# One macaron block on one core: the pool of norm vectors is opened before the two pools of split activations

## The chip, the core and the metric

The kernel runs on one core of a Trainium2 chip. The metric is device time in microseconds (us). The kernel before was run three times: 2274.84, 2276.01 and 2279.90 us, median 2276.01. A further execution was profiled; it took 2277.5 us, of which the profile's span of the program is 2275.7 us.

On this core PE multiplies matrices: a *stationary* operand of 128x128 is loaded into it (a weight load, PEld in the profile) and a *moving* operand of up to 512 columns streams past it. DVE, ACT and POOL work elementwise, SP issues DMAs. All five have their operands in the on-chip memory SBUF, in which a tile is a run of bytes at one address in each of 128 partitions; matmul results go to PSUM.

## The reference

For a float32 sequence of 1024 positions with 1024 features the reference computes one block:

```python
x = x + 0.5 * _swiglu(_rmsnorm(x, ffn1_norm[l]), ffn1_wg[l], ffn1_wu[l], ffn1_wd[l])
h = _rmsnorm(x, mix_norm[l])
proj = h @ w_in[l]
...
merged = gates[:, :, 0] * (y_a @ w_branch[l, 0])
... # the same for y_b, y_c, y_d
x = x + merged @ w_out[l]
x = x + 0.5 * _swiglu(_rmsnorm(x, ffn2_norm[l]), ffn2_wg[l], ffn2_wu[l], ffn2_wd[l])
```

`_swiglu` is `(silu(x @ wg) * (x @ wu)) @ wd` with 2816 inner features. `y_a` to `y_d` are four sequence mixers of width 256 (a gated linear recurrence in chunks, a retention, a windowed attention, and a convolution with a linear recurrence), each with its own projections in `w_in`; the rest of `w_in` gives the four gates.

## The kernel before

Every large product is made in three matmuls. A float32 operand is split into `hi`, the operand rounded to the type that PE multiplies fast (ACT), and `lo`, the rest (DVE or POOL); then hi·hi, hi·lo and lo·hi are summed in PSUM. Features lie in partitions, positions in columns, in two halves of 512 columns (q = 0, 1). One matmul has a 128x128 stationary piece of a weight and 512 columns of an activation as moving operand.

The program has three parts, one after the other.

- **FFN1** (class `Ffn`). The gate and up products are done by a scheme of seven block products instead of eight; their names are A11, A12, S2, S1, S4, A22 and S3 (`one`, lines 1160 to 1162). For each of 22 blocks of inner features, each name takes 4x3 matmuls; PE runs them in the order A11, S2, A12, S1, S4, A22, S3. The left operands (`xc_tiles`) of A11 and A12 lie in pool `h0`, those of S2 and S1 in pool `h1`, those of S4, A22 and S3 in pool `xc`. Weights come by DMA into `raw` and are split into `rg`, `rt`, `ru` and `v`. The finished activations are written to memory outside the core and come back for the down product (`down`, lines 1331 to 1333), both of whose split operands lie in `rg`, `rt` and `ru`; there 16 of the 24 raw weight loads go into `h0` and `h1`, since their left operands are dead by then.
- **The mixers and gates** (`mix`). The normed activation `h` (tiles nm0 and nm1, hi and lo) fills `h0` and `h1`. `unit` (lines 215 to 217) is 24 matmuls with a `w_in` piece from `rg`/`rt` as stationary and an `h` tile as moving operand. There are 56 pieces, each for both halves: 24 projections, then 32 gate pieces, each gate unit followed by 6 matmuls `wb` (lines 954 to 956) on the mixer's output, whose tiles lie in pools y0 and y1. The mixers themselves are generators in a background list: after each sixth matmul of a unit the list is ticked, and a generator whose count has run out issues its next step, with small matmuls of its own, between the unit's.
- **The output product and FFN2.** `product` (lines 260 to 262) multiplies the merged result, split again into `h0` and `h1`, by `w_out`: 384 matmuls with an `h0`/`h1` tile as moving operand. FFN2 is as FFN1.

PE's order is that of the code. The order of the other engines is that in which the pool and semaphore layer of the framework puts the program.

A pool is a stretch of SBUF; pools are stacked in the order in which they are opened. `const` starts at byte 16,512 of a partition and holds 2,176 bytes by the end (a packed table of 384, two columns of 64, three 128x128 tables of 512 each, 128 of derived vectors). `h0` and `h1` have eight buffers of 4,096 bytes each, so 65,536 together. `norm` holds the short vectors of the three norms: three tags (`rs_v`, `rs_y`, `rs_t`) of two buffers of 64 bytes, 384 in all. Then come `raw`, `rg` and `rt`, and after them the pools of each part. A tile of these has 4,096, 2,048 or 1,024 bytes, each a multiple of 512, so all tiles of one pool start at the same byte modulo 512:

| pool | starts at byte | modulo 512 |
|---|---|---|
| `const` | 16,512 | 128 |
| `h0`, `h1` | 18,688 | 256 |
| `norm` | 84,224 | 256 |
| `raw`, `rg`, `rt` | 84,608 | 128 |
| `v`, `t`, `s`, `xc`, `ru`, `tt`, `a`, `u`, `scale` of an FFN | 121,472 and up | 128 |
| y0, y1, merged, gate (with `wb`'s weights) | 144,000 and up | 128 |

Inside the pools of the four mixers some tiles are shorter, and their starts stand at other values (160, 224, 416 and more).

Of the kernel before, what the change touches and what calls it, by code (L numbers as in the profile page):

```python
# [34 lines left out]
class Weights:  # L35


    def __init__(self, nc, ahead):
        self.nc, self.ahead, self.alloc = nc, ahead, None
        self.src, self.got, self.lo_engine = [], {}, []  # L40
        self.issued = 0
# [51 lines left out]
class Net:  # L93
    def __init__(self, ctx, tc, a, cols):
        self.tc, self.nc, self.a = tc, tc.nc, a
        pool = lambda name, **kw: ctx.enter_context(tc.tile_pool(name=name, **kw))
        self.cpool = pool("const", bufs=1)
        self.hpools = [pool("h0", bufs=8), pool("h1", bufs=8)]
        self.npool = pool("norm", bufs=1)
        self.wide = {k: pool(k, bufs=b, reuse_waits="tile") for k, b in {"raw": 3, "rg": 4, "rt": 2}.items()}  # L100
        self.w, self.wo = Weights(self.nc, 2), Weights(self.nc, 2)
        self.w.alloc = self.wo.alloc = self.weight
        self.bg = Background()
        nc = self.nc
        self.small = self.const("small")
        self.mean_col = self.column("mean_col")
        nc.gpsimd.memset(self.mean_col, 1.0 / D)
        self.cols = cols
        self.eps = self.column("eps")
        nc.gpsimd.memset(self.eps, EPS)  # L110
# [1474 lines left out]
```

## Time and profile before

| | |
|---|---|
| median of three runs | 2276.01 us |
| the profiled execution | 2277.5 us, its span 2275.7 us |
| PE busy | 2220.4 us, 98% of the span, 10144 matmuls |
| PE weight loads busy | 1779.5 us, 78% |
| DVE busy | 1379.8 us, 61% |
| ACT busy | 875.5 us, 38% |
| POOL busy | 327.9 us, 14% |
| DMA queue q1 | 243.44 MB, 32% of 16 engines' span |

FFN1 takes the first 693 us, the projections run to 1011 us, the gates to 1523, the output product to 1612, FFN2 to the end. The ends of matmuls are modelled and overlap the next one's start, so how fast PE goes is read from the starts: the distance between the starts of two matmuls, divided by the number of matmuls between them.

### The profile page before, as it was taken

To read this page: it belongs to the slowest core of one execution; us is meant where nothing else is said; L and a number is where in the kernel's file an instruction comes from. 1 tells how busy PE (TensorE), PEld (TensorE's weight loads), DVE (VectorE), ACT (ScalarE), POOL (GpSimd) and SP (SyncE) were. 2 spreads that over 40 slices of the span, in tenths; PEclk is the share of its full clock that TensorE was granted. 3 is DMA by queue.
4 is the path that set the end of the run, shared out by engine and by line. 5 is a ranking of instruction groups with operands and counts; after the bars stand their busy time and mean duration, and the time that the engine had idled before them with its cause. 6 is when DMAs were issued, how large, how long until landed. Compare 5 with 4: busy or idle time off the path is not lost.

```text
span 2275.7 us, 26198 instructions
## 1 busy us (share of the span) xinstructions
PE 2220.4 (98%) x10144; PEld 1779.5 (78%) x10144; DVE 1379.8 (61%) x1925; ACT 875.5 (38%) x1154; POOL 327.9 (14%) x227
## 2 busy tenths in 40 slices
PE   6899999999999999999999999999999999999999
PEld 5688888887777777787777777888778888888777
DVE  8787777776673436314355233035788787777764
ACT  6232233233443533316477454133433333223332
POOL 0000000000003435223343344321100000000000
PEclk8999999999999999999999999999999999999999
DMA  3233232394333122231111222115223232348432
GB/s 142 93 102 106 86 111 91 124 325 149 106 125 112 53 75 78 77 117 65 58 54 45 74 72 88 47 47 181 79 93 115 93 116 93 116 135 318 139 115 93
DMA packets 115196, 245.10 MB, mean 108 GB/s; under 512 B 11264, under 2 KB 23168, under 8 KB 115072
## 3 DMA queue, kind: packets, MB, share of 16 engines
q1 hardware_dynamic: 115072, 243.44, 32.0%
q8 instruction: 79, 1.29, 0.2%
q14 instruction: 45, 0.37, 0.1%
HBM read 181.00 MB, written 62.39 MB: 107 GB/s over the span
## 4 chain that ended last, share of the span: by engine, by line
PE 91%; DVE 6%; ACT 2%; issue 1%; DMA 0%; POOL 0%; SPq 0%; DVEq 0%; ACTq 0%; POOLq 0%
PE X L1162 3%; PE X L1160 3%; PE X L1161 3%; PE S1p L1160 2%; PE S2p L1162 2%; PE S1p L1162 2%; PE S1p L1161 2%; PE S2p L1161 2%; PE S2p L1160 2%; PE S4p L1161 2%; PE S4p L1160 2%; PE S4p L1162 2%; PE S3p L1162 2%; PE S3p L1161 2%; PE A22p L1161 2%; PE S3p L1160 2%
## 5 line engine op out<-in xcount | busy, mean ns | idle before, releaser
L56 POOL TENSOR_TENSOR wlo<-raw,whi 128x1024 fp32r<-128x1024 f32 x56 | 136.4, 2438 | 258.3 <-ACT whi L55 246.7
L1011 ACT ACTIVATE uhi<-gu 128x1024 fp32r<-128x1024 f32 x44 | 46.7, 1062 | 276.4 <-PE S3p L1161 134.4
L55 ACT ACTIVATE whi<-raw 128x1024 fp32r<-128x1024 f32 x72 | 76.0, 1057 | 186.4 <-PE o L261 23.5
L964 DVE TENSOR_TENSOR gt<-gt,wb 128x512 f32<-128x512 f32 x48 | 32.9, 686 | 139.8 <-PE wb L956 80.0
L1011 ACT ACTIVATE ghi<-gu 128x1024 fp32r<-128x1024 f32 x44 | 46.7, 1060 | 164.4 <-DMA gu<-wgu 129.8
L191 POOL TENSOR_TENSOR nm0lo<-res,nm0hi 128x1024 fp32r<-128x1024 f32 x2 | 4.9, 2444 | 648.9 <-ACT nm0hi L190 648.9
L1160 PE MATMUL X<-A11hi,ghi 128*128 128x512 f32 x176 | 71.1, 404 | 9.3 <-ACT ghi L1011 9.3
L965 POOL TENSOR_TENSOR m<-m,gt 128x512 f32<-128x512 f32 x48 | 62.3, 1299 | 122.6 <-DVE gt L964 121.7
L1012 DVE TENSOR_TENSOR dloS<-wd,dhiS 128x1024 fp32r<-128x1024 f32 (+1 forms) x36 | 43.1, 1196 | 59.6 <-ACT dhiS L1011 59.6
L1160 PE MATMUL X<-A12hi,ghi 128*128 128x512 f32 x176 | 70.8, 402 | 7.7 <-ACT t L1170 7.7
L1162 PE MATMUL X<-A11hi,glo 128*128 128x512 f32 x176 | 71.5, 406 | 6.6 <-DVE glo L1012 6.6
L1011 ACT ACTIVATE dhiA<-wd 128x1024 fp32r<-128x1024 f32 (+1 forms) x36 | 35.6, 990 | 107.3 <-PE Ad L1332 53.4
L1011 ACT ACTIVATE dhiS<-wd 128x1024 fp32r<-128x1024 f32 (+1 forms) x36 | 35.6, 989 | 106.9 <-PE Dd L1332 39.1
L1162 PE MATMUL S2p<-S2hi,tlo 128*128 128x512 f32 x176 | 70.2, 399 | 4.2 <-DVE tlo L1012 4.2
L1206 ACT ACTIVATE a<-a 128x1024 f32<-128x1024 f32 x44 | 46.7, 1062 | 65.3 <-DVE a L1205 65.3
L1160 PE MATMUL S1p<-S1hi,thi 128*128 128x512 f32 x176 | 70.7, 402 | 0.0
L1161 PE MATMUL X<-A11lo,ghi 128*128 128x512 f32 x176 | 70.5, 401 | 0.0
L1162 PE MATMUL S1p<-S1hi,tlo 128*128 128x512 f32 x176 | 70.5, 400 | 0.0
L1161 PE MATMUL S1p<-S1lo,thi 128*128 128x512 f32 x176 | 70.4, 400 | 0.0
L1161 PE MATMUL X<-A12lo,ghi 128*128 128x512 f32 x176 | 70.4, 400 | 0.0
L1198 DVE TENSOR_TENSOR a<-S3p,a 128x512 f32<-128x512 f32 x44 | 30.4, 691 | 66.0 <-PE S3p L1162 66.0
L1332 PE MATMUL Ad<-aloA,dhiA 128*128 128x512 f32 x176 | 68.7, 390 | 1.6 <-DVE aloA L1012 1.6
(1209 smaller groups left out, 6895.1 us busy)
## 6 DMA issues: line engine op xcount, KB each, us to landing
gu<-wgu SPq DMA_DIRECT2D x92, 512.0 KB, 3.6
raw<-w_in SPq DMA_DIRECT2D x56, 512.0 KB, 3.5
acts<-s SPq DMA_DIRECT2D x88, 256.0 KB, 2.8
wd<-wd SPq DMA_DIRECT2D x40, 512.0 KB, 6.5
inS<-acts SPq DMA_DIRECT2D x40, 512.0 KB, 3.7
acts<-a SPq DMA_DIRECT2D x66, 256.0 KB, 3.3
inA<-acts SPq DMA_DIRECT2D x30, 512.0 KB, 3.7
res<-x SPq DMA_DIRECT2D x16, 512.0 KB, 7.1
```

The lines of the kernel that those rows point to most:

```text
L55: nc.scalar.activation(hi, raw, AF.Copy)
L56: getattr(nc, self.lo_engine[i]).tensor_tensor(lo, raw, hi.bitcast(F32), op=ALU.subtract)
L964: nc.vector.tensor_tensor(g, g, ps, op=ALU.mult)
L965: nc.gpsimd.tensor_tensor(m, m, g, op=ALU.add)
L1011: self.nc.scalar.activation(hi, src, AF.Copy)
L1012: self.nc.vector.tensor_tensor(lo, src, hi.bitcast(F32), op=ALU.subtract)
L1160: mm(ps, whi[:, s], hi, start=start and k == 0, stop=False, skip_group_check=True)
L1161: mm(ps, whi[:, s], lo, start=False, stop=False, skip_group_check=True)
L1162: mm(ps, wlo[:, s], hi, start=False, stop=k == 3, skip_group_check=True)
L1198: V.tensor_tensor(g[:, 1], ps, g[:, 1], op=ALU.add)
L1206: nc.scalar.activation(g, g, AF.Silu)
L1332: mm(outs[t], whi[:, j, m], alo[:, j], start=False, stop=False, skip_group_check=True)
```

## The change

One line moves: the pool `norm` is opened before `h0` and `h1` instead of after them.

```diff
         self.cpool = pool("const", bufs=1)
+        self.npool = pool("norm", bufs=1)
         self.hpools = [pool("h0", bufs=8), pool("h1", bufs=8)]
-        self.npool = pool("norm", bufs=1)
         self.wide = {k: pool(k, bufs=b, reuse_waits="tile") for k, b in {"raw": 3, "rg": 4, "rt": 2}.items()}
```

In the built program `norm` then starts at byte 18,688 and `h0` at 19,072, which is 128 modulo 512; `raw` and everything behind it keep their addresses. The instructions of all five engines are the same, in the same order and with the same waits. Only the addresses of tiles in `h0`, `h1` and `norm` differ: the first two by +384 bytes, the last by -65,536.

## Rows read from the trace of the kernel before

**Rows 1.** The page, parts 1 and 4: busy time; the chain that ended last.

```profile
PE 2220.4 (98%) x10144; PEld 1779.5 (78%) x10144; DVE 1379.8 (61%) x1925; ACT 875.5 (38%) x1154; POOL 327.9 (14%) x227
...
PE 91%; DVE 6%; ACT 2%; issue 1%; DMA 0%; POOL 0%; SPq 0%; DVEq 0%; ACTq 0%; POOLq 0%
```

**Rows 2.** Windows: stretch, length, busy us (instructions) by engine, granted clock, DMA share, GB/s.

```profile
0.00:105.00 105.00, 78.53 (x314) 62.28 (x314) 87.25 (x149) 54.58 (x69) 0.34 (x6) 0.89 0.32 115
105.00:470.00 365.00, 364.21 (x1580) 296.63 (x1581) 286.18 (x357) 106.59 (x131) 0.00 (x0) 1.00 0.34 116
...
693.00:1011.00 318.00, 313.88 (x1654) 246.11 (x1655) 125.56 (x258) 110.67 (x154) 117.74 (x73) 0.99 0.24 80
1011.00:1523.00 512.00, 511.68 (x2449) 399.95 (x2448) 182.93 (x337) 256.92 (x399) 185.21 (x138) 1.00 0.20 63
1523.00:1612.00 89.00, 89.00 (x383) 71.65 (x382) 46.74 (x50) 35.55 (x43) 11.89 (x5) 1.00 0.47 151
1612.00:1690.00 78.00, 70.71 (x321) 57.28 (x321) 68.10 (x91) 33.43 (x39) 5.13 (x2) 0.98 0.25 82
```

**Rows 3.** Timeline of PE in FFN1's gate and up: start us, us, instruction.

```profile
299.07 0.40 PE L1160 MATMUL S2p<-S2hi,thi 128*128 128x512 f32 x1
...
304.67 0.40 PE L1160 MATMUL S1p<-S1hi,thi 128*128 128x512 f32 x1
304.91 0.39 PE L1161 MATMUL S1p<-S1lo,thi 128*128 128x512 f32 x1
305.13 0.40 PE L1162 MATMUL S1p<-S1hi,tlo 128*128 128x512 f32 x1
...
307.47 0.39 PE L1160 MATMUL S4p<-S4hi,uhi 128*128 128x512 f32 x1
...
310.20 0.39 PE L1160 MATMUL A22p<-A22hi,vhi 128*128 128x512 f32 x1
...
315.64 0.40 PE L1160 MATMUL X<-A11hi,ghi 128*128 128x512 f32 x1
```

**Rows 4.** Timeline of PE in a gate unit and its wb.

```profile
1426.09 0.40 PE L215 MATMUL gb1q<-nm0hi,whi 128*128 128x512 f32 x1
...
1431.68 0.39 PE L954 MATMUL wb<-ybhi,wbhi 128*128 128x512 f32 x1
...
1433.06 0.40 PE L215 MATMUL gb1q<-nm1hi,whi 128*128 128x512 f32 x1
```

**Rows 5.** Timeline of PE in the output product.

```profile
1550.21 0.40 PE L260 MATMUL o<-mhi,whi 128*128 128x512 f32 x1
...
1560.01 0.40 PE L260 MATMUL o<-mhi,whi 128*128 128x512 f32 x1
```

**Rows 6.** Timeline of PE in FFN2's down product.

```profile
2102.63 0.39 PE L1331 MATMUL Bd<-ahiS,dhiS 128*128 128x512 f32 x1
...
2116.23 0.39 PE L1331 MATMUL Bd<-ahiS,dhiS 128*128 128x512 f32 x1
```

**Rows 7.** Window of one period of gate and up, PE alone: PE busy, granted clock, DMA.

```profile
300.00:318.90 18.90, 18.90 (x83) 1.00 0.24 71
```

**Rows 8.** Tiles S1lo and S3lo: PE's matmuls that read them, ns min/median/max.

```profile
L1161 PE MATMUL S1p<-S1lo,thi x176: 390/395/628, 45.5 to 2047.5; 128*128 128x512 f32 x176
...
L1161 PE MATMUL S3p<-S3lo,uhi x176: 389/389/389, 60.5 to 2055.6; 128*128 128x512 f32 x176
```

**Rows 9.** Waits of PE: waited for, us in total, times, longest.

```profile
PE vtr L419 <- DVE vst L412: 3.1, 1, 3.1
```

**Rows 10.** Groups of DVE by form, splits into h1 and xc: busy us, mean ns.

```profile
L1012 DVE TENSOR_TENSOR S1lo<-n1x,S1hi 128x1024 fp32r<-128x1024 f32 x2 | 2.4, 1219 | 0.0
...
L1012 DVE TENSOR_TENSOR S3lo<-n0x,S3hi 128x1024 fp32r<-128x1024 f32 x2 | 2.4, 1222 | 1.2 <-ACT S3hi L1011 1.2
```

**Rows 11.** Tile wd: what its readers waited for (us, times); its DMAs' landing.

```profile
  DMA wd<-wd: 0.7, 2
...
DMA to landing us min/median/max: 2.9/6.0/10.3
```

## The prediction

> **What bounds the kernel now.** I read the page first, then windows by stage, then PE's timeline in one place of each kind of product, and last the waits. The page says that PE is the bound: busy for 98% of the span, and 91% of the chain that ended last is PE [rows 1]. The windows say the same of each stage: PE fills 364 of 365 us of the steady gate and up, all but 0.3 us of the 512 us of gates and all 89 us of the output product, while DVE, the next busiest, has 286 of 365 us in the first of these [rows 2]. So nearly all of the time is a number of matmuls times the distance between their starts, and the question is only whether that distance depends on an address.
>
> The timeline answers it for the layout of before. In one period of gate and up, 36 matmuls of S2, A12 and S1 go from 299.07 to 307.47 us, 233.3 ns each; the 24 of A22 and S3 go from 310.20 to 315.64 us, 226.7 ns each [rows 3]. [...] The change of pace sits at the change of pool: S4, whose moving operand is in `xc` too, is the transition, 12 matmuls in 2.73 us or 227.5 ns. The other stages fall on the same two values. A gate unit, moving operand in `h0`/`h1`: 24 matmuls in 5.59 us, 232.9 ns; the six of `wb` behind it, all operands at 128: 1.38 us, 230.0 ns, a run too short to settle [rows 4]. The output product, moving operand in `h0`/`h1`: 42 in 9.80 us, 233.3 ns [rows 5]. The down product, all operands at 128: 60 in 13.60 us, 226.7 ns [rows 6]. The durations in the trace say it of all 176 matmuls of a group: S1lo has a median of 395 ns, S3lo is 389 at its least, median and most [rows 8].
>
> **The change part by part.** No instruction is added, removed or moved, and no wait; three pools change addresses, and each use of them is priced by itself.
>
> *Matmuls with a moving operand in `h0` or `h1`.* Of gate and up there are 4 names x 12 matmuls x 22 blocks x 2 FFNs = 2112; of units 56 x 2 x 24 = 2688; of the output product 384. Together 5184, half of the 10144. With `h0` and `h1` at 128, each of them has the residues that A22, S3 and the down product have now, so I give each their 226.7 ns.
>
> - Gate and up: 6.6 ns each. About 4 in 7 of the 635 matmuls in the two opening stretches (to 105 us, and from 1612 to 1690 us), some 360, gain nothing, since there PE is busy for only 78.5 of 105 and 70.7 of 78 us and waits for splits and norms, which do not become faster [rows 2]. That leaves 1750 x 6.6 ns = 11.6 us, and S4's transition adds 528 x 0.8 ns = 0.4 us. 12.0 us.
> - Units: 2688 x 6.2 ns = 16.7 us, and `wb` 64 x 6 x 3.3 ns = 1.3 us. Background work is issued behind at most every sixth matmul of a unit; a matmul with a small one next to it has no such distance to lose. I take half of these places as used and strike a twelfth: 16.5 us.
> - Output product: 384 x 6.6 ns = 2.5 us.
>
> The sum is 31.0 us. Struck from it: PE waits 3.1 us for a copy on DVE in front of a transpose [rows 9]. This wait ends when a chain on ACT, DVE and POOL ends, so what PE gains in the 40 us before it (some 170 matmuls x 6.2 ns = 1.0 us) only makes it longer. 30.0 us remain. Other waits of the mixers could grow as well, since their steps are spaced by counts of matmuls, and 36 matmuls become 0.2 us shorter. PE shows almost no waits there now: the gates' stage idles for 0.3 us in 512 [rows 2], so I take 0; with ends: none, or 30 places x 0.2 us = 6 us. A gain from this is excluded, as no step comes later.
>
> *DVE, ACT and POOL on tiles in `h0` and `h1`.* A split into `h1` takes DVE 1219 ns, one into `xc` 1222 ns [rows 10]: no difference between the residues. 0 us.
>
> *DMAs into `h0` and `h1`.* Of 48 loads of down weights, 32 go there. They land in 6.0 us at the median, and their readers sat idle for them for 0.7 us in all [rows 11]. I take 0; should they become slower, the down product's splits would be late first, and a twentieth on each landing (32 x 0.3 us = 10 us) would still be spread over loads that wait for nobody. With ends: -0.7 us, or +2 us if a fifth of it came through. [...]
>
> *Norm vectors.* They are a few columns wide and keep their residues. 0 us.
>
> [...]
>
> So the profiled execution of 2277.5 us would become 2247.5 us. The median of the runs shown is 1.5 us under that execution; from it, 2246 us.
>
> **The rivals.**
>
> *The pool matters, not the residue.* `h0` and `h1` are also the two pools lowest in the memory, and no other long moving operand lies there. If the 6 ns belong to that place, nothing happens: 2276 us, the change doing what it says to addresses and nothing to time. For it: the trace has no matmul of this shape at the bottom with residue 128, or higher up with 256. Against it: `h0` and `h1` reach over 64 KB and show one pace from end to end, and operands as far apart as `rg` (97 KB) and the FFN pools (from 121 KB) show another; a border just at the end of `h1` would be a coincidence. 7%.
>
> *The background work becomes the bound in the mixers.* The steps' spacing shrinks and PE runs into ACT and DVE chains; half of the units' 16.5 us is given back as waits in front of small matmuls, the time is 2254 us. For it: one such wait is there already [rows 9]. Against it: DVE has 126 of 318 and 183 of 512 us to do there [rows 2]. 8%.
>
> *The pairs lock in the slow step.* With `h` tiles the starts lie alternately 0.24 and 0.22 to 0.23 us apart [rows 3], as if each second matmul met something. If equal residues at the bottom of the memory made every matmul meet it, each of some 5000 would take up to 0.24 us, 6.7 ns more than now: +33 us, 2309 us. The point from which it decides is a mean distance in the units above 233 ns. Against it: all three products with equal residues show no alternation. 3%.
>
> **How the numbers follow.** The forecast (all `h` matmuls at the faster pace) has 82%, the rivals 7, 8 and 3%. The forecast's own spread is from 2241 us (nothing struck: 34.9 us) to 2252 us (6 us of grown waits). The second rival lies just above. A range from 2239 to 2258 us holds the forecast and the second rival but for their tails; the first and the third, 10%, stay outside. About 0.2% (4.5 us) is what a measurement of this kernel can tell from no change: faster has 90%, same 7%, slower 3%.
>
> **What would show it.** In the changed kernel's trace the groups S1p, S2p and X should have matmuls of 389 ns without spread; 36 matmuls from S2 to S4 should take 8.16 us instead of 8.40, a unit 5.44 instead of 5.59 us, 42 of the output product 9.52 instead of 9.80. The down product and A22/S3 should not change. PE's wait for the transpose should grow by about 1 us. If the distances in `h` products stay at 233 ns the first rival holds; if they fall and the gain is under 25 us, the waits of PE between 693 and 1523 us tell where it went. The prediction is wrong if the time is above 2258 us.

## The result, and the profile after

The changed kernel takes 2253.93 us (median of 4 runs, 2247.8 to 2257.39) against 2276.67 us (4 runs, 2274.84 to 2279.9): a ratio of 0.9896, interval 0.9870 to 0.9922. In the profiled executions the span goes from 2275.7 to 2254.2 us, 21.5 us less where 30 were forecast. The rest of the document is about these two numbers: with the time at the lower clock taken out 30.0 us are there, if not in the places where the sum had them, and 8.5 us go back to TensorE's clock. One of the 26 executions of the kernel before, beside the later experiments, took 12540 us; the ratios leave it out.

First the pace. PE's timeline of the changed kernel, the stretches of [rows 3 to 5] (start us, us, instruction):

```profile
295.76 0.39 PE L1160 MATMUL S2p<-S2hi,thi 128*128 128x512 f32 x1
...
303.92 0.39 PE L1160 MATMUL S4p<-S4hi,uhi 128*128 128x512 f32 x1
...
306.64 0.39 PE L1160 MATMUL A22p<-A22hi,vhi 128*128 128x512 f32 x1
...
312.08 0.39 PE L1160 MATMUL X<-A11hi,ghi 128*128 128x512 f32 x1
...
1416.75 0.39 PE L215 MATMUL gb1q<-nm0hi,whi 128*128 128x512 f32 x1
...
1422.19 0.39 PE L954 MATMUL wb<-ybhi,wbhi 128*128 128x512 f32 x1
...
1423.55 0.39 PE L215 MATMUL gb1q<-nm1hi,whi 128*128 128x512 f32 x1
...
1539.83 0.39 PE L260 MATMUL o<-mhi,whi 128*128 128x512 f32 x1
...
1549.35 0.39 PE L260 MATMUL o<-mhi,whi 128*128 128x512 f32 x1
```

The 36 matmuls from S2 to S4 take 8.16 us (8.40 in [rows 3]), the 24 of a unit 5.44 us (5.59 in [rows 4]), its `wb` 1.36 us (1.38), and 42 of the output product 9.52 us (9.80 in [rows 5]): 226.7 ns each. The 24 of A22 and S3 stay at 5.44 us. The spread of single durations has gone as well; the tiles S1lo and S3lo, ns min/median/max, against [rows 8]:

```profile
L1161 PE MATMUL S1p<-S1lo,thi x176: 387/389/628, 47.7 to 2025.9; 128*128 128x512 f32 x176
...
L1161 PE MATMUL S3p<-S3lo,uhi x176: 389/389/389, 59.5 to 2034.1; 128*128 128x512 f32 x176
```

Now what speaks against 30 us. The windows of the changed kernel, some of the stretches of [rows 2] (length; busy us and instructions of PE, PEld, DVE, ACT, POOL; granted clock, DMA share, GB/s):

```profile
105.00:470.00 365.00, 364.32 (x1607) 301.69 (x1608) 291.07 (x363) 108.76 (x134) 0.00 (x0) 1.00 0.36 121
693.00:1011.00 318.00, 313.24 (x1660) 247.44 (x1659) 123.61 (x256) 112.14 (x155) 116.32 (x73) 0.98 0.24 78
1011.00:1523.00 512.00, 511.35 (x2486) 406.62 (x2485) 187.12 (x340) 257.66 (x401) 184.52 (x139) 1.00 0.20 65
1612.00:1690.00 78.00, 75.07 (x335) 62.19 (x334) 64.79 (x92) 28.89 (x35) 0.00 (x0) 0.94 0.22 74
```

In steady gate and up, PE gets 1607 instructions done in 365 us where it did 1580, and in the gates 2486 where it did 2449. From 693 to 1011 us it is 1660 against 1654, hardly more, at a clock of 0.98 instead of 0.99. Windows of PE alone show where the clock was low; first before, then the changed kernel (PE busy us, granted clock):

```profile
693.50:697.00 3.50, 3.01 (x8) 0.61 0.92 264
1642.90:1646.00 3.10, 3.10 (x11) 0.54 0.00 0
1691.00:1694.50 3.50, 3.50 (x10) 0.52 0.60 177
```

```profile
654.90:661.60 6.70, 6.00 (x14) 0.50 0.63 188
781.20:784.50 3.30, 3.30 (x9) 0.50 0.04 16
859.70:863.00 3.30, 3.30 (x10) 0.50 0.44 117
900.70:904.00 3.30, 3.30 (x9) 0.50 0.45 164
1610.60:1614.00 3.40, 3.40 (x10) 0.50 0.00 0
1627.70:1634.30 6.60, 6.60 (x22) 0.50 0.00 0
```

In both traces the records of the granted clock hold 1.00 and 0.50 alone; they give these places 10.2 us at 0.50 before and 27.3 us after (the windows of before begin a little ahead of them, which is why they do not show 0.50; those of after lie inside them). The openings of the program, up to 75 us, have another 23.9 us of it in both. The timeline around the second place shows what PE did before the fall and what the low level costs:

```profile
776.09 0.39 PE L217 MATMUL p7q<-nm0hi,wlo 128*128 128x512 f32 x1
779.71 0.66 PE L419 MATMUL vtr<-c_ident,vst 128*128 128x128 f32 x4 [3.23 <-DVE vst L412]
...
781.55 0.63 PE L217 MATMUL p7q<-nm1hi,wlo 128*128 128x512 f32 x1
781.98 0.63 PE L215 MATMUL p7q<-nm1hi,whi 128*128 128x512 f32 x1
...
785.45 0.39 PE L216 MATMUL p7q<-nm1lo,whi 128*128 128x512 f32 x1
785.68 0.39 PE L217 MATMUL p7q<-nm1hi,wlo 128*128 128x512 f32 x1
```

PE idles for 3.23 us in front of the transpose, and 1.4 us after it has resumed the clock falls. The matmuls then start 0.43 us apart instead of 0.23. So a stretch at a granted clock of 0.50 in which PE has work costs about half its length. Ahead of the third place (the fourth reads alike) there is next to no wait, but a run of small matmuls:

```profile
855.84 0.39 PE L217 MATMUL p12q<-nm1hi,wlo 128*128 128x512 f32 x1
856.16 0.66 PE L488 MATMUL o<-Aatt,Av 128*64 128x128 f32 x8
856.65 0.26 PE L493 MATMUL o<-Aqbx,S 128*64 128x32 f32 x4
857.07 2.76 PE L493 MATMUL o<-Aqbx,S 128*64 128x32 f32 x27 [0.16 <-DVE S L475]
```

The wait for the transpose has grown, by 0.7 us where 1.0 was forecast ([rows 9]: 3.1 us, once):

```profile
PE vtr L419 <- DVE vst L412: 3.8, 2, 3.2
```

PE runs the same 10144 matmuls in the same order in both traces, so that stretches between equal matmuls can be compared. After minus before: FFN1's steady gate and up -6.1 us, the four groups of gates -2.4, -1.2, -2.1 and -2.7 us, the output product -2.6 us, FFN2's steady gate and up -7.4 us (1.5 us of it the fall at 1691 us, which only before has), both down products 0.0 us up to F, the last of FFN1's. Against that stand +2.8 us in F (the place at 655 us, 6.8 us of low clock), +1.5 us from the first `vtr` to p8 (781 us), +2.0 us in p12 (859 us) and +1.8 us in p15 (901 us). FFN2's opening stays as long as it was, with 10.2 us of low clock (1611 and 1628 us) where before had 3.4 us (1643 us).

### The profile page after: what moved, and what is told of

Read it like the earlier page. It is cut to its first block, busy times and chain, and to the rows that moved or that the text cites. A ratio compares the mean times of both kernels' runs of the same rounds, so it can differ in the third digit from the quotient of the medians.

```text
span 2254.2 us, 26198 instructions
## 1 busy us (share of the span) xinstructions
PE 2199.1 (98%) x10144; PEld 1783.1 (79%) x10144; DVE 1379.3 (61%) x1925; ACT 875.2 (39%) x1154; POOL 328.2 (15%) x227
## 4 chain that ended last, share of the span: by engine, by line
PE 88%; DVE 7%; ACT 3%; issue 1%; DMA 1%; POOL 0%; SPq 0%; DVEq 0%; ACTq 0%; POOLq 0%
PE X L1162 3%; PE X L1160 3%; PE X L1161 3%; PE S2p L1162 2%; PE S1p L1160 2%; PE S1p L1162 2%; PE S4p L1160 2%; PE S1p L1161 2%; PE S4p L1161 2%; PE S4p L1162 2%; PE S2p L1160 2%; PE S2p L1161 2%; PE S3p L1162 2%; PE A22p L1162 2%; PE S3p L1160 2%; PE A22p L1160 2%
## 5 line engine op out<-in xcount | busy, mean ns | idle before, releaser
L1160 PE MATMUL X<-A11hi,ghi 128*128 128x512 f32 x176 | 71.3, 405 | 10.2 <-ACT ghi L1011 10.2
L1162 PE MATMUL X<-A12hi,glo 128*128 128x512 f32 x176 | 69.7, 396 | 0.0
L1160 PE MATMUL S2p<-S2hi,thi 128*128 128x512 f32 x176 | 69.2, 393 | 0.0
```

The source lines that it names most:

```text
L1160: mm(ps, whi[:, s], hi, start=start and k == 0, stop=False, skip_group_check=True)
L1162: mm(ps, wlo[:, s], hi, start=False, stop=k == 3, skip_group_check=True)
```

## The experiments

half, all256, resid_a and vtr_later ran on one chip beside 9 runs of the kernel before (median 2276.93 us), resid_b, before_vtr and after_again on another beside 13 (2277.03 us). A mean distance of a name is taken from the start of its first matmul to the start of the next name's, over all periods of a steady stretch.

**half: one of the two pools.** The order of pools becomes `h1`, `norm`, `h0`; A11, A12 and nm0 live in `h0`, which now starts at 128 modulo 512, S1, S2 and nm1 in `h1`, which stays at 256.

```diff
-        self.hpools = [pool("h0", bufs=8), pool("h1", bufs=8)]
+        h1 = pool("h1", bufs=8)
         self.npool = pool("norm", bufs=1)
+        self.hpools = [pool("h0", bufs=8), h1]
```

> The changed kernel with h1 opened ahead of norm and h0 behind it: h0 at 128 modulo 512, h1 left at 256, everything else as before. Theory A (PE's pace depends on the starts of the moving and stationary operand modulo 512): products with operands in h0 (A11, A12, nm0 units, output product q=0) go at 227 ns from start to start, those in h1 (S2, S1, nm1 units, output product q=1) stay at 233 ns, and the time is halfway, about 2265 us (2276.7 before, 2253.9 with both). Theory B (the gain comes from something else that the move did, as the norm vectors' place or the order of the three pools): no such split between h0 and h1, both at 227 or both at 233 ns.

Measured: 2265.41 us (2264.91 to 2266.33), ratio 0.9949 (0.9937 to 0.9962), half-way between the two kernels. The groups by form from 106 to 446 us (busy us, mean ns of one) tell the pools apart in one kernel:

```profile
L1161 PE MATMUL S1p<-S1hi,thi 128*128 128x512 f32 x72 | 28.4, 394 | 0.0
...
L1161 PE MATMUL X<-A12hi,ghi 128*128 128x512 f32 x72 | 28.1, 390 | 0.0
L1161 PE MATMUL X<-A11hi,ghi 128*128 128x512 f32 x68 | 26.5, 389 | 0.0
...
L1161 PE MATMUL S2p<-S2hi,thi 128*128 128x512 f32 x71 | 28.0, 394 | 0.0
```

Mean distances: A11 226.7 and A12 228.1 ns (its first three matmuls, behind S2, are still slow), against S1 and S2 232.6 ns. The median unit on nm0 goes at 226.7 ns, on nm1 at 233.0 ns, and of the output product the first 192 matmuls (q = 0) at 226.7, the last 192 (q = 1) at 233.3 ns. `h0` now lies where `h1` lay before, and where S1 and S2 were slow A11 and A12 are fast. That speaks against the place; whether 256 is itself a slow start is left to the next kernel.

**all256: equal, but at 256.** 128 bytes of padding behind `norm` put every operand pool, the weights too, at 256 modulo 512.

```diff
         self.npool = pool("norm", bufs=1)
+        pool("pad", bufs=1).tile([P, 32], F32, tag="pad", name="pad")
```

> The changed kernel with a pad of 128 bytes between norm and h0, so that h0, h1 and every later pool (weights, xc, y, the mixers' too) start at 256 modulo 512 where the changed kernel has 128. Theory A1 (what counts is the difference between moving and stationary operand): differences are 0 as in the changed kernel, all products at 227 ns, time as the changed kernel's, about 2254 us. Theory A2 (what counts is the moving operand's own start: 128 is good and 256 is bad): all 512-column products at 233 ns, those of xc and down too, about 4,500 more than before at +6.6 ns: 2276 + 30 = 2306 us.

Measured: 2252.44 us (2248.01 to 2256.67), ratio 0.9898 (0.9883 to 0.9913), the same as the changed kernel. All names of gate and up run at 226.7 ns, S1 as A22:

```profile
L1161 PE MATMUL S1p<-S1hi,thi 128*128 128x512 f32 x72 | 28.0, 389 | 0.0
...
L1161 PE MATMUL A22p<-A22hi,vhi 128*128 128x512 f32 x72 | 28.0, 389 | 0.0
```

So 256 is no slow start for a moving operand, and the bottom of the memory no slow place: what counts is how the two starts stand to each other.

**resid_a and resid_b: how unequal.** Padding ahead of FFN pools shifts the weights of A22 by `a` bytes and those of S3 and S4 by `b` against the `h` and `xc` pools; other weights keep their start. The diff is resid_a's; resid_b has (32, 480) for FFN1 and (192, 448) for FFN2. Each was run once.

```diff
+        a, b = {1: (64, 128), 2: (256, 384)}[n]
+        def shifted(k, bufs):
+            by = {"v": a, "t": 512 - a, "ru": b, "tt": 512 - b}.get(k)
+            if by:
+                pool("pad" + k, 1).tile([P, by // 4], F32, tag="pad", name="pad" + k)
+            return pool(k, bufs)
```

> The changed kernel with the weights of two groups moved by pads: stationary operands of A22 (pool v) start 64 bytes later modulo 512 in FFN1 and 256 later in FFN2, those of S4 and S3 (pool ru, also the stationary of every second down step) 128 later in FFN1 and 384 later in FFN2; all moving operands stay at 128. Theory A1 (difference counts): S3 of FFN1, difference 128 as in the kernel before but with the sign turned and in pools far above h0, leaves 227 ns for about 233; the other three differences show how the price depends on the distance. Theory A2 (the moving operand's own start counts): all four stay at 227 ns. Total: 264 matmuls a group and FFN at up to +6.6 ns, at most +10 us on the changed kernel.

> As resid_a with other distances of the stationary operand's start, moving operands at 128: A22 +32 bytes in FFN1 and +192 in FFN2; S4, S3 and every second down step +480 (that is -32) in FFN1 and +448 (-64) in FFN2. In resid_a +64 cost 6.3 ns, +128 6.4, +384 6.3 and +256 3.2 ns a matmul. Theory A1 as a matter of equal or not: +32, +192, -32 and -64 cost about 6 ns as well. Theory A1 as a matter of distance: +-32 costs less than half of +-64.

Measured: 2265.98 us and 2258.29 us; the mean distances, by how far the stationary operand's start lies behind the moving one's, modulo 512:

| bytes | 0 | 32 | 64 | 128 | 192 | 256 | 384 | 448 | 480 |
|---|---|---|---|---|---|---|---|---|---|
| ns | 226.7 | 232.6 | 232.9 | 233.1 | 228.9 | 229.8 | 233.0 | 228.9 | 232.9 to 233.3 |

resid_a's timeline, one period of FFN1 (A22 at 64, S3 and S4 at 128), and of FFN2 A11 (at 0, behind S3), S4 (at 384) and A22 (at 256, behind S4):

```profile
307.08 0.40 PE L1168 MATMUL S4p<-S4hi,uhi 128*128 128x512 f32 x1
...
309.88 0.40 PE L1168 MATMUL A22p<-A22hi,vhi 128*128 128x512 f32 x1
...
312.67 0.39 PE L1168 MATMUL S3p<-S3hi,uhi 128*128 128x512 f32 x1
...
315.47 0.39 PE L1168 MATMUL X<-A11hi,ghi 128*128 128x512 f32 x1
...
1810.84 0.40 PE L1168 MATMUL X<-A11hi,ghi 128*128 128x512 f32 x1
...
1812.45 0.39 PE L1169 MATMUL X<-A11lo,ghi 128*128 128x512 f32 x1
...
1813.36 0.39 PE L1170 MATMUL X<-A11hi,glo 128*128 128x512 f32 x1
...
1821.75 0.40 PE L1168 MATMUL S4p<-S4hi,uhi 128*128 128x512 f32 x1
...
1824.55 0.40 PE L1168 MATMUL A22p<-A22hi,vhi 128*128 128x512 f32 x1
...
1826.17 0.39 PE L1169 MATMUL A22p<-A22lo,vhi 128*128 128x512 f32 x1
...
1827.07 0.40 PE L1170 MATMUL A22p<-A22hi,vlo 128*128 128x512 f32 x1
```

The 229.8 ns at 256 are no cost of 256. The seven first matmuls of A22 take 1.62 us behind S4, and the seven first of A11, whose two starts are equal, take 1.61 us behind S3; the four distances after them are 0.90 and 0.91 us long, 225 to 228 ns each, and over all periods 227 ns for both names. So A22 at 256 settles where A11 at 0 does, and its mean is raised by the transition alone. The other seven inequalities cost 2.2 to 6.6 ns of 226.7, and the size goes with the distance modulo 256 wherever two of them agree in it: 0 and 256 cost nothing, 128 and 384 cost 6.4 and 6.3 ns, 192 and 448 both 2.2 ns. By this 448 is the case of 192 and not of 64 (6.2 ns), 480 that of 224. These are three pairs in one execution each. Of the expectations those that have the moving operand's own start or the plain distance decide fell, and so did "equal or not", by 256, 192 and 448. Why 192 costs less than 32, 64 or 128 stays open. The layout of before is the case of 384 (moving at 256, weights at 128).

**vtr_later: the changed kernel without its longest wait.** The steps that transpose values are spaced by counts of PE's matmuls; the first of them comes six places later, so that DVE's copy is done when PE reaches the transpose. In the changed kernel PE waits 0.6 and 3.2 us (by its list of waits) ahead of two of these transposes, and 1.4 us behind the longer wait its granted clock falls to 0.50.

```diff
     def a_values(self, st, q, ft):
-        yield 3
+        yield 9
```

> The changed kernel with the pause ahead of mixer A's four value transposes raised from 3 to 9 ticks, nothing else. [...] Theory S1 (part of what is missing from the forecast's 30 us went into this wait and the clock behind it): the wait goes, 4 to 6 us faster than the changed kernel, about 2249 us. Theory S2 (the time is given back elsewhere, since the chain of DVE, ACT and POOL that ends there also starts mixer A): the wait moves to mixer A's first transposes and the time stays within 2 us of the changed kernel's.

Measured: 2238.95 us (2238.41 to 2243.37), ratio 0.9837 (0.9823 to 0.9850): 15 us below the first four runs of the changed kernel, 12 us below its four later ones (after_again), and the fastest of all. Both waits are gone, and so is every low clock between 692 and 1596 us; a shorter wait is new there:

```profile
PE ds L469 <- ACT Akd L518: 1.3, 1, 1.3
```

Windows of PE from 764 us, the changed kernel and then this one:

```profile
764.00:800.00 36.00, 32.21 (x143) 0.95 0.17 51
800.00:900.00 100.00, 99.62 (x609) 0.98 0.23 74
900.00:1008.00 108.00, 108.00 (x581) 0.98 0.25 88
```

```profile
764.00:800.00 36.00, 36.00 (x168) 1.00 0.24 81
800.00:900.00 100.00, 98.64 (x631) 1.00 0.24 76
900.00:1008.00 108.00, 108.00 (x586) 1.00 0.28 98
```

Of the 17.1 us between the two profiled spans, 11.3 us lie between the first projection and the first gate (the three low stretches of the changed kernel there, 10.2 us, cost about 5.1; one at 688 us of vtr_later, 3.4 us, takes 1.7 back), 2.8 us in FFN1's F and 3.4 us in FFN2's opening. The last two places are not touched by the edit; with the clock taken out they differ by 0.6 us or less. Even the larger expectation, 4 to 6 us, was too small: the falls at 859 and 901 us and the two other places were not in it.

**before_vtr: the same delay in the layout of before.** It tells whether those 15 us belong to the delay or to the layout.

> The kernel before (h0, h1 at 256 modulo 512) with mixer A's value transposes 9 instead of 3 ticks later, as in vtr_later. There the later transposes took 15 us off the changed kernel. Theory S1 (the changed kernel lost part of its 30 us to this wait and to the clock that falls behind such waits; the kernel before had the wait, but not the falls): here the delay is worth less than there, 5 to 10 us, about 2269 us, and the distance to vtr_later (2239.0) is 30 us, the forecast's. Theory S2 (the two changes have nothing to do with each other): the delay is worth the same 15 us here, 2262 us, and the distance stays at 23 us.

Measured: 2272.06 us (2269.83 to 2276.91), ratio 0.9978 (0.9968 to 0.9989). The delay is worth 5.0 us here, the lower end of theory S1's 5 to 10; between the first projection and the first gate it is 5.7 us, with one low stretch of 3.4 us at the start of it in each trace. Between this kernel and vtr_later, in which neither has that wait, the layout is worth 33.1 us by medians (taken on two chips, on which the kernel before agrees to 0.1 us) and 34.0 by spans.

**after_again: the changed kernel once more.**

> The changed kernel once more, to see what differs between executions of one program. Theory S1 (the missing 7 us are time at the lower granted clock behind short waits, which does or does not come in one execution): the runs spread over 2247 to 2258 us in the order of their mean granted clock, about 4 us for each 0.001, and a profile with a clock of 0.992 shows the forecast's 30 us. Theory S2 (the missing time is in waits that each execution has): the runs lie closer together than the 7 us, whatever their clock.

Measured: 2250.99 us (2250.79 to 2256.82), ratio 0.9889 (0.9874 to 0.9904). With its first four the changed kernel has eight runs; four with a mean clock of 0.991 took 2247.8 to 2251.88 us, one with 0.990 2251.13 us, two with 0.989 2255.98 and 2256.82 us, one with 0.988 2257.39 us. The same program, with the same instructions and addresses, thus spreads over 9.6 us, and the order of its times is that of the clock it was granted, but for steps of 0.001. In this profile the places of low clock are 776, 895, 1606 and 1623 us; those at 655 and 859 us do not come again.

## Why the prediction was right, and where it was not

*Pace by the residue: right.* What the layout is worth can be read with the clock taken out: the span less half of the time at a granted clock of 0.50 (up to PE's last matmul).

| kernel | span us | at clock 0.50 us | span less half |
|---|---|---|---|
| before | 2275.7 | 34.1 | 2258.6 |
| after | 2254.2 | 51.2 | 2228.6 |
| after_again | 2249.1 | 41.0 | 2228.6 |
| all256 | 2246.2 | 34.1 | 2229.2 |
| half | 2263.6 | 37.6 | 2244.8 |
| before_vtr | 2271.1 | 41.0 | 2250.6 |
| vtr_later | 2237.1 | 34.1 | 2220.0 |

After is 30.0 us below before, all256 29.4, half 13.8, and vtr_later is 30.6 below before_vtr. Three executions with equal starts come within 0.6 us of each other, although their spans differ by 8 us. (Where PE waits anyway, as in the openings, half is an upper end: FFN1's opening has 3.4 us more of low clock in vtr_later than in before_vtr and is 0.1 us longer, so 1.6 of the 30.6 us are too much.)

The prediction took its two paces, 233.3 and 226.7 ns, from one period of before, with a granted clock of 1.00 over the whole of it [rows 7]. The weight pools differed in it as well (`rg` and `rt` for the slow names, `v` and `ru` for the fast ones, all at 128), so that trace alone did not tell the activations' pool from the weights'. The change did, as the weights stayed where they were.

*The terms of the sum: two of three right, and the total in part by luck.* After minus before by stage, in us:

| stage | forecast | measured | with the clock taken out |
|---|---|---|---|
| steady gate and up of both FFNs | -12.0 | -13.5 | -12.0 |
| projections and gates, with `wb` and waits | -15.5 | -8.3 | -11.7 |
| output product | -2.5 | -2.6 | -2.6 |
| F of FFN1's down product | 0 | +2.8 | -0.6 |
| FFN2's opening | 0 | +0.1 | -3.1 |
| sum | -30.0 | -21.5 | -30.0 |

The projections and gates give 3.8 us less than the sum had. Of two unit matmuls in sequence, away from low clock, the distance shrank by 5.1 ns in the mean (2548 distances); 6.2 ns less a twelfth would be 5.7, so more than a twelfth of them had little to lose. And distances that a small matmul takes part in grew by 2.7 us where 1.0 us was struck. FFN2's opening, which was to gain nothing, makes up for it: in all256, with as much low clock there as before, it is 3.4 us shorter outright. How much of that is the layout's isn't settled, as with the clock out it is 1.9 us shorter in before_vtr too.

*The wait for `vst`: right in sign and size.* 3.1 us became 3.2 us and a second of 0.6 us, so 0.7 us more for the 1.0 us of the sum.

*The term that was missing: the clock.* The other waits, taken as 0, stayed small: those new in the mixers are 0.6 us once in front of nm1ms and 0.4 us in front of `o`, within the ends given. What the sum had no term for is the clock. I had read it as 1.00 in steady stretches and took the 0.99 from 693 to 1011 us as given. In the profiled executions the time at a granted clock of 0.50 went from 34.1 to 51.2 us, which costs 8.5 us at half its length; 30.0 - 8.5 = 21.5 us is the difference of the spans. The 2253.93 us lie above the forecast's own spread, which ended at 2252 us, and in the range only by the room that it left for the second rival: as far as the clock goes that was luck. The other profile of the same kernel has 41.0 us, 3.4 us of cost and a difference of 26.6.

*The rivals.* Place: fell by the pace of the changed kernel, whose `h0` and `h1` are still at the bottom, and by half. Slow step: fell by the pace. Background work as the bound: it had the right place in part (three of the six places of low clock, 10.2 of 27.3 us, are in the mixers) and the right size (2254 us), but mostly another mechanism: the larger part of what is missing is a lower clock, the smaller the 2.7 us of distances with small matmuls. With the longest wait gone the falls at 859 and 901 us were gone too; that the wait caused them isn't shown, since the steps behind it moved as well.

*DVE, DMA, norms: 0, not contradicted.* The down products, which read what the DMAs into `h` bring, are unchanged to 0.03 us where the clock is. These loads land in 6.0 and 6.2 us at the median in before and before_vtr, in 6.3 to 7.0 us in the three profiles with `h` at 128 (after, after_again, vtr_later), and in 6.5 us in all256 with `h` back at 256: no cost of the start can be told from this, and their readers waited for them for 1.2 us at most.

What stays open: why the clock falls more often in the faster layout. It isn't settled that it does, by any rule: the mean clock is 0.990 to 0.994 in the first nine runs of before beside the experiments, 0.988 to 0.991 in eight of after, 0.988 to 0.992 in all256, and without the long wait 0.992 to 0.993 in vtr_later, but 0.988 to 0.993 in before_vtr. So neither the layout nor the wait puts them in order. What the traces show is that the wait of 3.2 us for `vst` has a fall of the clock beside it, from 1.2 us before its end to 1.4 us after it, in all six profiles of changed layouts that have it (half, all256, resid_a, resid_b, after, after_again), and that the one of 3.1 us in before has none. Nor was it settled why the delay gains 5.7 us where the wait was 3.1 us; the steps behind it move too.

## What to carry to other kernels

Where PE is the bound, compare the distance between starts of equal matmuls across stages: here two values at one clock came from where the two operands start, and pools whose starts agree modulo 512 were worth 30 us of 2276 at equal clock (23 to 26 us as measured) for 384 bytes of shift. Take the clock out (span less half of the time at a granted clock of 0.50) before a forecast of a per cent is judged, and look at it again after any gain on PE, since moving one step, for which PE waited 3 us, gave 12 to 15 us here in the new layout and 5 us in the old one.

## What the runs showed that was not expected

The cost of unequal starts is not one size, starts 256 bytes apart cost nothing once the pace has settled, and the sizes repeat with 256 bytes in the pairs that were run. And a single execution of one program can differ by 9.6 us from another: 2257.39 us at a mean clock of 0.988, 2247.8 us at 0.991, with small waits and small matmuls of the same program ahead of the falls in some executions and not in others.
